# Two MLPs of a small encoder: weight halves made five steps ahead, and one partial product kept in PSUM

## The chip, the core and the metric

The kernel runs on one core of a Trainium2 chip. Five engines work side by side, each through its own instructions in order: TensorE (PE in the profile, its weight loads PEld), VectorE (DVE), ScalarE (ACT), GpSimd (POOL) and SyncE (SP), which here only issues DMA transfers. TensorE writes into PSUM, which has eight banks; DVE and ACT read it from there. The metric is the device time of one execution in microseconds (us). Three runs of the kernel before took 1002.46, 1002.76 and 1003.22 us, so the median is 1002.76 us.

## The reference

Two layers on one sequence of 512 rows with 1024 features, all in fp32. Layer 0 mixes the rows by stick-breaking attention, layer 1 by a gated linear recurrence; each is followed by the same kind of MLP, and a last normalisation ends it:

```python
for layer in range(2):
    h = rms_norm(x, norm_mix[layer])
    x = x + (stick_breaking_attention(h, ...) if layer == 0 else rglru_block(h, ...))
    h = rms_norm(x, norm_mlp[layer])
    u = relu(h @ mlp_w1[layer])            # 1024 -> 4096
    x = x + (u * u) @ mlp_w2[layer]        # 4096 -> 1024
return rms_norm(x, norm_final)
```

The change touches only the two MLPs.

## The kernel before

**Three products for one.** A matrix product in fp32 is made of three in fp32r. An operand `a` is cut into a high half `ah`, which is `a` rounded to fp32r, and a low half `al = a - ah`; the product is `ah*wh + ah*wl + al*wh`. For each tile of weights, then, ACT makes `wh` with a cast and DVE makes `wl` with a subtraction. In the profile these are the groups `ACT CAST wh<-b` and `DVE TENSOR_TENSOR wl<-b,wh`, both of line 798, the line of the helper through which the MLP issues to ACT and DVE.

**Seven products for eight.** Each MLP is cut into four quarters of the 4096 inner features. Quarter 0's first product is done plainly (`squared`); everything after it goes through the fast scheme with seven block products instead of eight, named P1 to P7, for both products of the MLP ("up": 1024 to 4096, "down": 4096 to 1024). The method `run` lists all of it as steps: for quarters 1 to 3, 14 up steps (two parts `p`, seven products each), and for each quarter 14 down steps (seven products, two parts `g` each). That is 98 steps for each MLP. An up step is 24 matmuls of 256 columns (line 1036), a down step 12 matmuls of 512 columns (line 1135).

The down steps come in an order written out by hand:

```python
"mid":  "P1 0 P5 0 P1 1 P2 0 P5 1 P6 0 P6 1 P3 0 P3 1 P7 0 P7 1 P2 1 P4 0 P4 1",
"last": "P1 0 P5 0 P1 1 P2 0 P5 1 P2 1 P6 0 P6 1 P3 0 P3 1 P7 0 P7 1 P4 0 P4 1",
```

"last" is for the fourth quarter of the second MLP alone.

**Sums in PSUM.** Products go to three sums. X takes P1, P6, P7 and P4 one on top of the other, and it is read between them: after P1 it is worth one block of the output, after P6 another, and so on. So TensorE may write P6 only when X has been read after P1. V takes P5 and then P3 in the same manner, W takes P2 alone. In the up steps a sum is one bank and ACT copies it out (`u<-ps`); in the down steps it is two banks (the two halves of a block of rows), and `collect` adds each, scaled, to the output tile `c` (the group `SCALAR_TENSOR_TENSOR c<-ps`). The banks come in a fixed cycle of eight, `BANKS = "oottaazz"` (tags o, t, acc and z, two banks each).

**The operands of the steps.** The weights come in blocks `b11`, `b12`, `b22` in six tiles `b`, loaded by SP's queue one stage ahead at fixed steps (`load`), and `b21` in a tile `raw` just for P2 (`source`). The operand of P5 is `b11 + b12` and that of P6 is this plus `b22`, each added in place by DVE (`DVE b L798`); that of P7 and of P4 is formed by a DMA that adds in flight, issued by POOL (line 1113). `operand` makes `wh` and `wl` from the block, in one of four pairs of tiles. `added` forms a sum, `add(n, ahead)` says how many steps ahead it may be done (P5 two; P6 one in the up steps, none in the down steps, where P6 of part 0 goes by DMA instead), and `make` makes an operand.

**What sets the order.** Within `run`, ACT and DVE execute in exactly the order in which the program writes their instructions (`Ordered`); TensorE too. After each step `i` the program writes `leave(i)`: it reads out the sum of step `i`, and calls `prepare(i + 4)`, which makes the operand that is four steps ahead. For up steps it also squares the result and splits it into halves for the down steps: `u` is combined by DVE (`u<-u`), goes through Relu and Square on ACT, is cast (`sh` or `bh`) and subtracted (`sl` or `bl`). In `leave` of a down step with part 1, the order is: collect the first bank, do the addition for the operand that is `ahead`, collect the second bank, then prepare. Three splits (`waiting`) are put off to fixed places in the down stage. A step's place is its number in the quarter: 0 to 13 up, 14 to 27 down.

**Tiles that matter here.** `wpool` has four buffers each of `wh` and `wl`, and three of `raw`. `raw` is used by P2 inside `run`, and before and after it by the plain slabs (`slab`), among them the first three of the recurrence's input projection, right behind the first MLP.

Of the kernel before, what the change touches and what calls it, by code (L numbers as in the profile page):

```python
# [13 lines left out]
F32R = mybir.dt.float32r  # L14
# [53 lines left out]
def hybrid_encoder(  # L68
# [739 lines left out]
    class Mlp:  # L808
# [28 lines left out]
        def __init__(self, ctx, layer):  # L837
            self.layer, self.sq, self.first = layer, Squares(), None
            self.V, self.A = Ordered(V), Ordered(A)
            self.mp = ctx.enter_context(tc.tile_pool(name=f"mlp{layer}", bufs=2))  # L840
            self.c = [
                self.mp.tile([P, 2, S], F32, tag=f"c{i}", name=f"c{i}", bufs=1) for i in range(4)
            ]
            self.begun, self.a, self.aside = set(), {}, {}
            self.turns = count(4 * layer)
            self.blocks = ExitStack()
            self.bp = self.blocks.enter_context(tc.tile_pool(name=f"blocks{layer}", bufs=2))
            self.u, self.lows, self.s3, self.slots = {}, {}, {}, None

            t = self.bp.tile([P, C // 2 * S + ASIDE], F32R, tag="s41", name="s41", bufs=1)  # L850
            self.s41 = t[:, : C // 2 * S].rearrange("p (k s) -> p k s", s=S)
# [5 lines left out]
        def bank(self):  # L857
            tag = self.BANKS[next(self.turns) % 8]
            return bank("acc" if tag == "a" else tag)
# [231 lines left out]
        def operand(self, raw):  # L1091
            pool = wpools[next(slabs) % len(wpools)]
            wh = pool.tile([P, C, P], F32R, tag="wh", name="wh")
            wl = pool.tile([P, C, P], F32R, tag="wl", name="wl")
            wh, wl = (t.rearrange("p (j k) f -> p j (k f)", j=2) for t in (wh, wl))
            self.A.copy(wh, raw)
            self.V.tensor_tensor(wl, raw, f(wh), ALU.subtract)
            return wh, wl
# [62 lines left out]
        def part(self, sums, name, g, w):  # L1161

            to = self.PRODUCTS[name][3]
            if to not in sums:
                sums[to] = [self.bank() for _ in range(2)]
            for i in range(2):
                self.times(name, g, i, w, sums[to][i], name in ("P1", "P5", "P2"))
# [4 lines left out]
        def run(self, first, between, end):  # L1172
# [47 lines left out]
            def prepare(i):  # L1220
# [5 lines left out]
                if i < len(steps) and steps[i][0] == "down":  # L1226
                    add(i, 0)
                    if waiting and place(i) in (20, 22, 23):
                        self.split_slot(*waiting.pop(0))
# [8 lines left out]
            def load(i):  # L1238
                q4, at = steps[i][1], place(i)
                for do in self.aside.get(i, ()):  # L1240
                    do()

                if i == 0:
                    self.turns = count(2)
                elif at == 0:
                    self.turns = count(4)
                    self.u.clear()
                    del self.a[1]
                elif at == 4:
                    units["down", q4] = self.from_down(q4)  # L1250
                    self.load(units["down", q4], (0, "b11"), (0, "b12"), (1, "b11"))
                elif at == 11:
# [3 lines left out]
                elif at == 22 and q4 < NQ - 1:  # L1256
                    units["up", q4 + 1] = self.from_up(q4 + 1)
                    self.load(units["up", q4 + 1], (0, "b11"), (0, "b12"), (0, "b22"), (1, "b11"))
                elif at == 25 and q4 < NQ - 1:
                    self.load(units["up", q4 + 1], (1, "b12"), (1, "b22"))  # L1260

            def leave(i):

                ahead = i + 4
# [4 lines left out]
                if kind == "down":  # L1269
                    if q4 == 0 and self.s3 and place(i) in self.REPLACE:  # L1270
                        self.replace()
                    apart = p and name == "P2" and self.layer and q4 == NQ - 1
                    if p and not apart:
# [3 lines left out]
                    if p and not apart:  # L1277
# [132 lines left out]
    with ExitStack() as mctx:  # L1410
# [18 lines left out]
        def end(ws, xs):  # L1429
            x_down(0, 0)  # L1430
            for i in range(2):
# [3 lines left out]
                if i == 0:  # L1435
                    for c in range(4, C):
                        feature(c, "zzoo"[c - 4])
# [457 lines left out]
```

## Time and profile before

| | |
|---|---|
| median of three runs | 1002.76 us |
| profiled execution | 1003.18 us |
| its span, first to last instruction | 1001.3 us |
| granted TensorE clock | 0.999 |
| busy: PE, PEld, DVE, ACT, POOL | 98%, 88%, 86%, 71%, 18% of the span |
| up and down steps of quarters 1 to 3, first MLP | 320.8 to 545.1 us of the span |
| the same, second MLP | 766.6 to 991.7 us |

A row of the timeline gives the start, the duration, the engine, the line, the operation, the tiles written and read, how many, and in brackets how long the engine stood idle just before and what ended it. Durations of neighbours overlap a little: an instruction's own time is the distance from its start to that of the next. So two `wl` in a row, shown together as 2.35 us with 1.22 us each, take 1.14 us apiece of DVE's queue, and the matmuls of 512 columns, shown with 379 ns, come every 216 ns.

### The profile page before, as it was taken

Reading aid. Unit: us, or ns where it says so; the run is one execution under the profiler, and the core shown is the slowest. Engines: PE = TensorE matmul, PEld = TensorE weight load, DVE = VectorE, ACT = ScalarE, POOL = GpSimd, SP = SyncE. Lnnn points to the kernel's source line nnn. Section 1 sums busy time; section 2 is a strip of 40 time slices with the busy share of each in tenths; the row PEclk is TensorE's granted clock in tenths of the full one; section 3 lists DMA queues with packets and bytes.
Section 4 is the critical chain, followed back from the end, with each engine's and each line's share of the span. In section 5 each row is a group of like instructions: output and inputs, shape, how many; then the busy total and the mean of one; then the engine's idle time right before and its main releaser. Section 6 shows DMA issues by size and latency. Waiting matters only on the chain.

```text
span 1001.3 us, 15918 instructions
## 1 busy us (share of the span) xinstructions
PE 983.0 (98%) x5836; PEld 884.0 (88%) x5836; DVE 858.0 (86%) x1152; ACT 715.4 (71%) x1110; POOL 176.4 (18%) x243
## 2 busy tenths in 40 slices
PE   9999999999999999999999999999999999999996
PEld 7889999888878988988988888888889989989985
DVE  6888787848898799799799799986887898998898
ACT  6777676836887774774775699975887774874865
POOL 0454444420000011011011220100011111111111
PEclk9999999999999999999999999999999999999999
DMA  7855454537637767777693474446548877977953
GB/s 230 216 146 148 106 153 109 160 117 256 174 87 198 169 160 198 169 163 194 169 239 88 128 191 126 124 157 223 122 95 219 212 142 202 249 141 199 229 107 106
DMA packets 71902, 165.72 MB, mean 166 GB/s; under 512 B 23824, under 2 KB 25104, under 8 KB 71824
## 3 DMA queue, kind: packets, MB, share of 16 engines
q1 hardware_dynamic: 59424, 123.54, 39.4%
q0 software_dynamic: 11680, 40.38, 24.0%
q8 instruction: 46, 0.75, 0.3%
q10 hardware_dynamic: 720, 0.79, 0.2%
q14 instruction: 32, 0.26, 0.1%
HBM read 139.51 MB, written 6.29 MB: 146 GB/s over the span
## 4 chain that ended last, share of the span: by engine, by line
PE 39%; DVE 25%; ACT 22%; issue 8%; DMA 6%; SPq 0%; ACTq 0%; POOL 0%; DVEq 0%; POOLq 0%
PE ps_t L1135 8%; DVE wl L798 6%; ACT wh L798 6%; PE ps_acc L1135 4%; DVE u L798 4%; ACT u L798 3%; PE ps_acc L1036 3%; DVE b L798 3%; PE ps_acc L257 3%; PE ps_acc L259 3%; PE ps_acc L258 2%; PE ps_z L1135 2%; ACT bh L798 2%; DVE c L798 2%; ACT L798 2%
## 5 line engine op out<-in xcount | busy, mean ns | idle before, releaser
L798 ACT CAST wh<-b 128x1024 fp32r<-128x1024 f32 x168 | 173.7, 1048 | 99.6 <-DVE b L798 50.1
L798 DVE TENSOR_TENSOR wl<-b,wh 128x1024 fp32r<-128x1024 f32 x168 | 203.6, 1220 | 38.9 <-ACT wh L798 38.5
L1113 POOL DMA_DIRECT2D b<-in_w_dn x40 | 35.0, 876 | 339.6 <-DVE b L798 153.1
L1036 PE MATMUL ps_z<-xg,wh 128*128 128x256 f32 x384 | 78.2, 277 | 1.0 <-ACT u L798 1.0
L257 PE MATMUL ps_acc<-xg,wh 128*128 128x512 f32 x200 | 79.1, 395 | 0.0
L259 PE MATMUL ps_acc<-xg,wh 128*128 128x512 f32 x200 | 75.8, 379 | 0.0
L258 PE MATMUL ps_acc<-xg,wl 128*128 128x512 f32 x200 | 75.8, 379 | 0.0
L251 DVE TENSOR_TENSOR wl<-raw,wh 128x512 fp32r<-128x512 f32 (+2 forms) x70 | 62.0, 911 | 15.1 <-ACT wh L249 14.8
L798 ACT ACTIVATE u<-u 128x512 f32<-128x512 f32 x100 | 63.2, 632 | 13.3 <-DVE u L798 11.6
L623 DVE TENSOR_TENSOR_SCAN scan<-keep,later 128x128 f32<-128x128 f32 (+1 forms) x64 | 59.3, 929 | 12.9 <-ACT keep L613 6.5
L1036 PE MATMUL ps_z<-xg,wl 128*128 128x256 f32 x240 | 66.0, 275 | 0.0
L1036 PEld LDWEIGHTS ps_z<-xg,wh 128*128 128x128 f32 x384 | 63.5, 192 | 1.7 <-ACT u L798 1.6
L249 ACT CAST wh<-raw 128x512 fp32r<-128x512 f32 (+2 forms) x70 | 50.5, 757 | 19.1 <-PE ps_acc L259 6.8
L627 POOL TENSOR_TENSOR w<-w,scan 128x128 f32<-128x128 f32 (+1 forms) x64 | 51.6, 807 | 53.6 <-DVE scan L623 50.6
L1036 PE MATMUL ps_acc<-xg,wh 128*128 128x256 f32 x288 | 60.5, 275 | 0.0
L798 DVE TENSOR_TENSOR b<-b,b 128x1024 f32<-128x1024 f32 x48 | 58.7, 1223 | 1.3
L798 DVE TENSOR_TENSOR u<-u 128x512 f32<-128x512 f32 (+1 forms) x92 | 54.8, 595 | 2.3 <-ACT u L798 1.0
L1113 POOL DMA_DIRECT2D b<-in_w_up x24 | 20.9, 869 | 196.8 <-DMA b<-in_w_up 84.4
L1036 PE MATMUL ps_acc<-xg,wl 128*128 128x256 f32 x192 | 52.8, 275 | 0.0
L1036 PE MATMUL ps_acc<-low,wh 128*128 128x256 f32 x192 | 52.8, 275 | 0.0
L798 ACT CAST wh<-raw 128x1024 fp32r<-128x1024 f32 x46 | 47.9, 1043 | 4.1 <-PE ps_acc L1135 4.0
L1135 PE MATMUL ps_t<-wh,sl 128*128 128x512 f32 x126 | 48.5, 385 | 1.9 <-DVE sl L798 1.9
(372 smaller groups left out, 3257.9 us busy)
## 6 DMA issues: line engine op xcount, KB each, us to landing
b<-in_w_dn SPq DMA_DIRECT2D x48, 512.0 KB, 5.1
b<-in_w_dn POOLq DMA_DIRECT2D x40, 512.0 KB, 5.5
b<-in_w_up SPq DMA_DIRECT2D x36, 512.0 KB, 4.7
b<-in_w_up POOLq DMA_DIRECT2D x24, 512.0 KB, 5.8
raw<-in_w_m SPq DMA_DIRECT2D x16, 512.0 KB, 4.7
raw<-in_w_dn SPq DMA_DIRECT2D x16, 512.0 KB, 4.9
raw<-in_w_in SPq DMA_DIRECT2D x16, 512.0 KB, 4.2
raw<-in_w_qk SPq DMA_DIRECT2D x12, 512.0 KB, 3.7
```

The source lines that it names most:

```text
L249: A.copy(wh[:, k, :], raw[:, k, :])
L251: V.tensor_tensor(wl[:, k, :], raw[:, k, :], f(wh[:, k, :]), ALU.subtract)
L257: PE.matmul(ps, wh, ah, start=start, stop=False)
L258: PE.matmul(ps, wl, ah, start=False, stop=False)
L259: PE.matmul(ps, wh, al, start=False, stop=stop)
L623: V.tensor_tensor_scan(sc[:, S - n : S][:, ::-1], keep[:, :n][:, ::-1], later[:, S - n :][:, ::-1], 1.0, ALU.mult, ALU.max,)
L627: G.tensor_tensor(wt, wt, sc[:, S - n + 1 : S + 1], ALU.mult)
L798: ins = getattr(self.e, name)(*args, **kwargs)
L1036: PE.matmul(as_read(ps[:, i * HS : (i + 1) * HS]), m, turns_of(y), start=new and i == k == n == 0, stop=i == 1 and k == C // 2 - 1 and n == 2,
L1113: G.dma_start(out=unit[b].rearrange("p j n -> p (j n)"), in_=unit["src"](to), accum_op=ALU.add)
L1135: PE.matmul(ps, m, y[:, jj], start=first and n == 0, stop=last and n == 2, skip_group_check=not new,)
```

## The change

Three things, all inside the MLPs.

1. **Five steps ahead.** From step 14 on (the first up step of quarter 1) `leave(i)` prepares the operand of step `i + 5` and not `i + 4`. The loads of the `b` tiles, from there on, are issued one step sooner. The put-off splits keep the step at which they are written. A fifth pair of tiles for halves is needed: every operand whose number divides by five, from 15 on, uses a fixed pair, `spare`, whose two tiles are two of the three `raw` buffers, held to the end of the MLP. P2's loads are left with one.
2. **W stays in PSUM.** The two banks of the down steps' W are taken once (`kept`) and P2 of all four quarters accumulates there. The collects of P2 in quarters 0, 1 and 2, two each, are gone; only the last quarter's remain.
3. **A plan of banks.** The other six banks are given out by a list written for each quarter (`planned`), X and V of the ups and downs in the order in which they are first used; `self.turns` starts elsewhere for the plain products before, and two transposes behind the first MLP use banks acc and t where it was o twice.

```diff
@@ Mlp.__init__, bank
-            self.turns = count(4 * layer)
+            self.kept, self.growing = None, False
+            self.planned = []
+            self.turns, self.operands, self.spare = count(2 + 2 * layer), count(), None
...
-            tag = self.BANKS[next(self.turns) % 8]
+            tag = self.planned.pop(0) if self.planned else self.BANKS[next(self.turns) % 8]
@@ operand
-            pool = wpools[next(slabs) % len(wpools)]
-            wh = pool.tile([P, C, P], F32R, tag="wh", name="wh")
-            wl = pool.tile([P, C, P], F32R, tag="wl", name="wl")
+            n = next(self.operands)
+            if n >= self.STEPS // 2 and n % 5 == 0:
+                if self.spare is None:
+                    self.spare = [
+                        wpool.tile([P, C, P], F32R, tag="raw", name="spare", bufs=3) for _ in range(2)
+                    ]
+                wh, wl = self.spare
+            else:
+                wh = wpool.tile([P, C, P], F32R, tag="wh", name="wh")
+                wl = wpool.tile([P, C, P], F32R, tag="wl", name="wl")
@@ part
             if to not in sums:
-                sums[to] = [self.bank() for _ in range(2)]
+                if to == "W":
+                    self.kept = self.kept or [self.bank() for _ in range(2)]
+                sums[to] = self.kept if to == "W" else [self.bank() for _ in range(2)]
+            new = name in ("P1", "P5") or name == "P2" and not self.growing
+            self.growing = self.growing or name == "P2" and g == 1
             for i in range(2):
-                self.times(name, g, i, w, sums[to][i], name in ("P1", "P5", "P2"))
+                self.times(name, g, i, w, sums[to][i], new)
@@ run: prepare, load, leave
-                    if waiting and place(i) in (20, 22, 23):
+                    if waiting and place(i) in (21, 23, 24):
...
+                sooner = i >= self.STEPS // 2
                 if i == 0:
-                    self.turns = count(2)
+                    self.planned[:] = "ooatzz"
                 elif at == 0:
-                    self.turns = count(4)
+                    self.planned[:] = ("", "atatooaatoat", "totoaattoa", "oaoattooatat")[q4]
...
-                elif at == 4:
+                elif at == 4 - sooner:
...
-                elif at == 11:
+                elif at == 11 - sooner:
...
-                elif at == 22 and q4 < NQ - 1:
+                elif at == 22 - sooner and q4 < NQ - 1:
...
-                elif at == 25 and q4 < NQ - 1:
+                elif at == 25 - sooner and q4 < NQ - 1:
...
-                ahead = i + 4
+                ahead = i + (5 if i >= self.STEPS // 2 else 4)
...
+                    grows = name == "P2" and q4 < NQ - 1
-                    if p and not apart:
+                    if p and not apart and not grows:
                         self.collect(name, 0, bank[0])
                     if steps[min(ahead, len(steps) - 1)][0] == "down":
                         add(ahead, 0)
-                    if p and not apart:
+                    if p and not apart and not grows:
                         self.collect(name, 1, bank[1])
                     prepare(ahead)
@@ end of the first MLP
-                        feature(c, "zzoo"[c - 4])
+                        feature(c, ("z", "z", "acc", "t")[c - 4])
```

## The prediction

> **What bounds the kernel now.** I read the page first, then the windows of single quarters, TensorE's waits, and last the timelines of TensorE, DVE and ACT in the third quarter of the first MLP, the one from 396.31 us on.
>
> ```profile
> span 1001.3 us, 15918 instructions
> ...
> PE 983.0 (98%) x5836; PEld 884.0 (88%) x5836; DVE 858.0 (86%) x1152; ACT 715.4 (71%) x1110; POOL 176.4 (18%) x243
> ```
>
> ```profile
> core 0: us, PE busy (x) PEld busy (x) DVE busy (x) ACT busy (x) POOL busy (x), PEclk, DMA share, GB/s
> ...
> 396.31:471.05 74.74, 74.33 (x505) 68.96 (x504) 67.25 (x74) 49.13 (x62) 7.85 (x9) 1.00 0.72 177
> ...
> 842.77:917.70 74.93, 74.52 (x506) 69.04 (x505) 69.07 (x77) 49.32 (x62) 10.45 (x12) 1.00 0.84 197
> ```
>
> ```profile
> PE ps_t L1135 <- DVE sl L798: 1.9, 6, 0.3
> PE ps_acc L1135 <- DVE wl L798: 1.4, 3, 0.6
> ...
> PE ps_z L1036 <- ACT u L798: 1.0, 3, 0.6
> ```
>
> TensorE is the bound: it is busy for 74.3 of the 74.7 us of a quarter, at full clock. There is little to win, then. DVE, at 67.3 of 74.7 us, is the next, and its 7.5 us of idle time lie in the first half of the quarter, so in the second half it is a bound of its own. The six waits for `sl` are one in each of the six quarters 1 to 3.
>
> What they cost is seen in the starts of the matmuls around them, and the chain of waits gives the start of P6:
>
> ```profile
> 431.15 0.28 PE L1036 MATMUL ps_z<-xg,wh 128*128 128x256 f32 x1
> ...
> 433.83 0.38 PE L1135 MATMUL ps_t<-wh,bh 128*128 128x512 f32 x1
> ...
> 439.25 0.38 PE L1135 MATMUL ps_t<-wl,sh 128*128 128x512 f32 x1
> 439.95 0.48 PE L1135 MATMUL ps_t<-wh,sl 128*128 128x512 f32 x1 [0.32 <-DVE sl L798]
> 440.27 0.38 PE L1135 MATMUL ps_t<-wh,sh 128*128 128x512 f32 x1
> ...
> 442.21 0.38 PE L1135 MATMUL ps_z<-wh,bh 128*128 128x512 f32 x1
> 442.68 0.48 PE L1135 MATMUL ps_z<-wl,bh 128*128 128x512 f32 x1
> 443.00 0.38 PE L1135 MATMUL ps_z<-wh,bl 128*128 128x512 f32 x1
> ```
>
> ```profile
> 447.91 5.18 PE ps_t L1135 x24
> ...
> 471.22 0.89 PE ps_acc L1036 x8
> ```
>
> 24 matmuls in 5.18 us are 0.216 us each. From 439.25 to 440.27 two take 1.02 us and not 0.43: a wait shown as 0.32 costs 0.59, its own length and 0.27 to get going again. From 442.21 to 443.00 the second wait (P2's `wl`) costs 0.36 likewise. So **0.95 us of each of these quarters, 5.7 us in all**, is what the change can take away at the start of the down stages. The down stage begins at 433.83 (P1 of part 0); P1 of part 1 two steps later at 439.0; P6 at 447.91; the up stage's last step, P4, at 431.15.
>
> **The change, part by part.** *The queue of DVE.* The order on DVE and ACT is the program's, so moving each operand one step ahead moves it past the work of one `leave`. These are DVE's rows from the start of its busy stretch, and ACT's beside them:
>
> ```profile
> 418.30 1.76 DVE L798 TENSOR_TENSOR bl<-u,bh 128x1536 fp32r<-128x1536 f32 x1 [1.47 <-ACT bh L798]
> ...
> 431.42 1.23 DVE L798 TENSOR_TENSOR b<-b,b 128x1024 f32<-128x1024 f32 x1
> ...
> 436.21 0.68 DVE L798 TENSOR_TENSOR u<-u,ps_o 128x512 f32<-128x512 f32 x1
> 436.81 1.22 DVE L798 TENSOR_TENSOR wl<-b,wh 128x1024 fp32r<-128x1024 f32 x1
> 438.06 1.23 DVE L798 TENSOR_TENSOR b<-b,b 128x1024 f32<-128x1024 f32 x1
> 439.21 0.69 DVE L798 TENSOR_TENSOR sl<-u,sh 128x512 fp32r<-128x512 f32 x1
> 440.06 1.42 DVE L798 TENSOR_TENSOR u<-u 128x512 f32<-128x512 f32 x2 [0.17 <-ACT u L798]
> 441.40 1.22 DVE L798 TENSOR_TENSOR wl<-raw,wh 128x1024 fp32r<-128x1024 f32 x1
> ...
> 443.74 2.35 DVE L798 TENSOR_TENSOR wl<-b,wh 128x1024 fp32r<-128x1024 f32 x2
> 446.01 0.74 DVE L798 SCALAR_TENSOR_TENSOR c<-ps_t,rr,c 128x512 f32<-128x512 f32 x1
> 446.68 1.21 DVE L798 TENSOR_TENSOR b<-b,b 128x1024 f32<-128x1024 f32 x1
> ```
>
> ```profile
> 428.67 0.59 ACT L798 COPY u<-ps_z 128x512 f32<-128x512 f32 x1 [0.28 <-PE ps_z L1036]
> ...
> 432.68 1.06 ACT L798 CAST wh<-b 128x1024 fp32r<-128x1024 f32 x1 [0.45 <-DVE b L798]
> ...
> 436.93 1.30 ACT L798 ACTIVATE u<-u 128x512 f32<-128x512 f32 x2 [0.40 <-DVE u L798]
> 438.26 0.62 ACT L798 CAST sh<-u 128x512 fp32r<-128x512 f32 x1
> 438.78 0.59 ACT L798 ACTIVATE u<-ps_z 128x512 f32<-128x512 f32 x1
> ```
>
> At 418.30 DVE has just waited: nothing is queued, and this point hangs on the up steps alone, so it stays. From there I write the queue anew, with 1.14 us for each `wl` and each addition and 0.60 for each `sl` and `u`, from the distances of the rows.
>
> (a) *P4 up.* The operand of P5 (part 0) with its addition is now written before ACT's copy of X after P7, the row at 428.67. The addition of 431.42 goes ahead of one `bl` (1.14) and one `u` (0.60), and the `wl` that followed 418.30 is already made (1.14), so it starts near 428.5. ACT's cast must wait for its end, 429.8, takes 0.95, and the copy runs from 430.75 to 431.3. P4 adds onto the same bank and wants to start at 431.15: 0.2 late, with the 0.27 some **0.5 us** (0 to 1).
>
> (b) *P1 of part 1.* The addition of 438.06 (P5's, part 1) now lies before the `u` of 436.21, which starts at 437.35, and with 0.2 of waits for ACT near 437.5. Between this `u` and the `sl` of 439.21 stands Relu, Square and cast: 436.21 to 438.88, that is 2.67 us. In their shadow DVE had 0.60 + 1.14 + 1.14 us of work; without the addition only 1.74, and it idles for 0.95. `sl` runs then from 440.25 to 440.95, where TensorE, unstopped but for (a), needs it at 439.45 + 0.5. That is 1.0 late, **1.2 us** with the new start (0.9 to 1.5). P2's `wl`, a step early now, is in time: its 0.36 goes.
>
> (c) *P6 of part 0.* P6 adds onto X, so both collects of P1 come first, the rows from 446.01 on. Before, the order was collect, addition for P6 of part 1, collect, then its operand. Now the addition and the operand belong to the `leave` before, in front of the first collect. An addition followed by its cast and `wl` with nothing between stands in the last quarter:
>
> ```profile
> 971.30 1.22 DVE L798 TENSOR_TENSOR b<-b,b 128x1024 f32<-128x1024 f32 x1
> 973.71 1.22 DVE L798 TENSOR_TENSOR wl<-b,wh 128x1024 fp32r<-128x1024 f32 x1 [1.19 <-ACT wh L798]
> ```
>
> So ahead of the collect DVE has the same number of `wl` as before (one more here, one less behind 418.30), one addition more (1.14), and these waits: 1.2 for this cast, 0.95 of (b), 0.6 for the sums behind ACT's Relu and Square of 438.78 to 440.04 (0.17 before, when less `sh` lay behind), 0.7 elsewhere against 0.61. The waits grow by 2.7, the collect starts at 446.01 + 1.14 + 2.7 = 449.85 and ends at 450.6. TensorE reaches P6 at 447.91 - 0.95 + 0.5 + 1.2 = 448.65: 1.95 late, **2.2 us** with the new start. Bounds: 0, if half of the 3.8 us is made good; 3.5, the addition, cast and `wl` in full.
>
> A quarter with the "mid" order: 0.5 + 1.2 + 2.2 - 0.95 = **+2.95 us**, five times 14.7. In the last quarter of the second MLP P2 of part 1 stands before P6, 2.6 us more room, so (c) falls away: 0.5 + 1.2 - 0.95, **+0.5** taken (0 to 1.5), as two shorter waits for `wl` there may go too.
>
> *W kept in PSUM.* Twelve collects go, in six pairs. The pair of this quarter, and ACT's cast beside it:
>
> ```profile
> 467.62 1.40 DVE L798 SCALAR_TENSOR_TENSOR c<-ps_z,rr,c 128x512 f32<-128x512 f32 x2
> 468.94 1.22 DVE L798 TENSOR_TENSOR wl<-b,wh 128x1024 fp32r<-128x1024 f32 x1
> ```
>
> ```profile
> 467.81 1.04 ACT L798 CAST wh<-b 128x1024 fp32r<-128x1024 f32 x1 [3.28 <-DVE b L798]
> ```
>
> The pair takes 1.32 us, but the `wl` behind it needs the cast that ends at 468.85: without the pair DVE would idle there as long. Worth 0. If that cover were gone it would give 1.3 us a quarter, 8 in all.
>
> *The plan of banks.* The trace shows no wait for a bank given anew; the three for `ACT u` are X's, read between two products on one bank. Six banks serve ten sums of a quarter, each first written several steps after its previous reader: 0, at worst 0.6 + 0.27 in each quarter, 5. [...]
>
> *One `raw` buffer.*
>
> ```profile
> raw<-in_w_dn SPq DMA_DIRECT2D x16, 512.0 KB, 4.9
> ```
>
> A load of P2 can now start only when the P2 before is subtracted. These lie five steps (13 us) or more apart, against 4.9 for the load: 0. In the "last" order they are two steps apart and ACT may wait some 2 us, which TensorE needs three steps later: 0, at most 2. Behind the first MLP the second input slab's `raw` is a spare tile, free when P2 of part 1 has run; two steps of 2.6, sixteen transposes and the load's 4.9 with cast and `wl` (2.2) end about together: 0 to 1.
>
> **Sum:** 14.7 + 0.5 = +15.2 on the profiled execution's 1003.18 (its span 1001.3 and 1.9 around it), 1018.4; this execution lies 0.4 above the median of 1002.76, so **1018 us**.
>
> **Rivals.**
>
> *The gaps close (faster).* If weights one step early and 1.3 us less of DVE work a quarter let DVE enter the down stage early enough, all of 5.7 us goes, and with the three waits for `ACT u` (1.0 + 0.8) up to 7.5: 995 to 997. The point: collect (c) must start by 446.9, not 449.85, so 3 us of my 3.8 must be wrong. For it: the same gap in every quarter; against it: the wait in (b) is for `sl`, which is not made earlier. [...]
>
> *Half of it.* (c) comes to nothing because the collects are in time, (a) and (b) stay: 0.75 a quarter, +4.3, 1007.
>
> *Worse.* The single `raw` buffer or SP's queue behind it holds up ACT in each quarter as it may in the last: 2 us more in five of them, 1028.
>
> *No effect.* Both sides cancel, or the fifth pair is not free before the steps need it, so that ACT waits as before: 1002 to 1004.
>
> **How the numbers follow.** Forecast with its own range 1012 to 1022: 0.66. Half: 0.12. Worse: 0.07. No effect: 0.06. Gaps close: 0.09. The range of 8 in 10 reaches to the half case and covers the bounds of (c): 1006 to 1023. About 0.2%, 2 us, is what a measurement of this kernel tells from no change. Faster by more: 0.09; within: 0.05; slower: 0.86.
>
> **What would show it.** Right: in the third quarter's down stage TensorE waits before P6 for `DVE c` with about 2 us, a row that is not there before; `sl` of P1 is waited for longer, P2's `wl` no more; ACT's copy `u` stops P4 up; a quarter of 74.7 becomes 77.7; DVE idles about 3.5 us between its 418.30 and the first collect. Wrong: quarters under 74.7, the row `b<-b,b` still behind the first `c<-ps_t`, or the added time lying outside quarters 1 to 3.

## The result and the profile after

The changed kernel takes 1027.39 us, the median of four runs (1025.44 to 1031.72), beside 1002.78 for the kernel before. The ratio is 1.0253, with a 95% interval from 1.0236 to 1.027. The profiled execution took 1025.44, with a span of 1023.5 us; the kernel before had 1001.3, so the two traces differ by 22.2. The page after:

```profile
span 1023.5 us, 15900 instructions
...
PE 989.1 (97%) x5836; PEld 888.9 (87%) x5836; DVE 852.6 (83%) x1140; ACT 712.3 (70%) x1110; POOL 176.1 (17%) x243
```

DVE has twelve instructions less (1140 for 1152), the collects of W, and is busy 5.4 us less. TensorE has the same 5836 matmuls, and its busy time has grown by 6.1, so not all of the loss stands in the rows as idle time.

The windows of quarters 1 and 2, of the first MLP and then of the second. Two of the four stand in the prediction as they were before, 74.74 and 74.93:

```profile
core 0: us, PE busy (x) PEld busy (x) DVE busy (x) ACT busy (x) POOL busy (x), PEclk, DMA share, GB/s
320.17:400.27 80.10, 75.42 (x505) 69.33 (x504) 66.64 (x72) 51.07 (x65) 7.81 (x9) 1.00 0.70 170
400.27:478.07 77.80, 74.82 (x505) 69.11 (x504) 66.36 (x72) 48.61 (x62) 7.85 (x9) 1.00 0.70 170
779.26:861.51 82.25, 77.03 (x505) 70.44 (x504) 68.32 (x74) 51.32 (x65) 9.69 (x12) 0.98 0.77 184
861.51:939.75 78.24, 74.83 (x506) 69.11 (x505) 67.71 (x75) 48.68 (x62) 10.42 (x12) 1.00 0.81 188
```

Quarter 2 is 3.06 and 3.31 longer than before. Quarter 1 is longer still, by 4.63 and 6.04 (75.47 and 76.21 before), and in one of the four the granted clock is 0.98.

TensorE's waits, in us in total, how often, and the longest:

```profile
PE ps_t L1144 <- DVE c L798: 4.1, 2, 2.0
PE ps_acc L1144 <- DVE c L798: 4.1, 2, 2.0
PE ps_acc L1038 <- ACT u L798: 3.7, 6, 0.8
PE ps_o L1144 <- DVE c L798: 2.7, 2, 2.0
PE ps_t L1038 <- ACT u L798: 1.9, 2, 1.0
PE ps_t L1144 <- ACT sh L798: 1.3, 2, 0.6
PE ps_acc L1144 <- ACT sh L798: 1.3, 2, 0.6
PE ps_o L1144 <- ACT sh L798: 1.3, 2, 0.6
...
PE ps_o L1038 <- ACT u L798: 1.0, 2, 0.7
```

Line 1144 is the down step now, 1038 the up step. The six rows of `c` and `sh` are new. Five of the six waits for `c` are 2.03 long and stand before P6, one in each quarter with the "mid" order; the six for `sh` stand before P1 of part 1; and the waits for `ACT u`, three of 1.0 in all before, are ten with 6.6. The late start at P2's `wl` is gone. (The rows for `wl` that remain are not P2's: they stand in the two quarters 0, which are still four ahead. A wait for `c` of 0.67 is new in the last quarter.)

DVE in the third quarter of the first MLP, the one that the prediction rewrote (its 418.30 is the 422.22 here):

```profile
422.22 1.76 DVE L798 TENSOR_TENSOR bl<-u,bh 128x1536 fp32r<-128x1536 f32 x1 [1.48 <-ACT bh L798]
...
437.65 0.69 DVE L798 TENSOR_TENSOR sl<-u,sh 128x512 fp32r<-128x512 f32 x1 [0.29 <-ACT sh L798]
438.61 1.23 DVE L798 TENSOR_TENSOR wl<-b,wh 128x1024 fp32r<-128x1024 f32 x1 [0.27 <-ACT wh L798]
439.87 1.23 DVE L798 TENSOR_TENSOR b<-b,b 128x1024 f32<-128x1024 f32 x1
...
444.30 0.69 DVE L798 TENSOR_TENSOR sl<-u,sh 128x512 fp32r<-128x512 f32 x1 [0.87 <-ACT sh L798]
445.46 1.42 DVE L798 TENSOR_TENSOR u<-u 128x512 f32<-128x512 f32 x2 [0.47 <-ACT u L798]
...
450.28 1.22 DVE L798 TENSOR_TENSOR b<-b,b 128x1024 f32<-128x1024 f32 x1
452.66 1.23 DVE L798 TENSOR_TENSOR wl<-b,wh 128x1024 fp32r<-128x1024 f32 x1 [1.17 <-ACT wh L798]
453.80 1.40 DVE L798 SCALAR_TENSOR_TENSOR c<-ps_t,rr,c 128x512 f32<-128x512 f32 x2
```

Both collects now stand behind the addition of 450.28, its cast on ACT and its half. The waits in brackets add up to 3.07 (0.78 before). The first collect starts 31.58 after the `bl` of 422.22, where it was 27.71 before: 3.87 later, 1.14 of it the third addition and 2.73 waiting. (The brackets alone give 2.29 of the 2.73, since they leave out the stretch by which neighbouring rows overlap, and waits too short to be listed.)

### The profile page after: what moved, and what is told of

Read it like the earlier page. It is cut to its first block, busy times and chain, and to the rows that moved or that the text cites. A ratio compares the mean times of both kernels' runs of the same rounds, so it can differ in the third digit from the quotient of the medians.

```text
span 1023.5 us, 15900 instructions
## 1 busy us (share of the span) xinstructions
PE 989.1 (97%) x5836; PEld 888.9 (87%) x5836; DVE 852.6 (83%) x1140; ACT 712.3 (70%) x1110; POOL 176.1 (17%) x243
## 4 chain that ended last, share of the span: by engine, by line
PE 42%; DVE 23%; ACT 18%; issue 9%; DMA 6%; SPq 0%; ACTq 0%; POOL 0%; DVEq 0%; POOLq 0%
DVE wl L798 6%; ACT wh L798 4%; PE ps_t L1144 4%; DVE b L798 3%; PE ps_acc L257 3%; PE ps_acc L259 3%; PE ps_acc L258 3%; ACT u L798 3%; PE ps_o L1144 3%; PE ps_o L1038 3%; PE ps_acc L1144 3%; DVE u L798 2%; PE ps_t L1038 2%; DVE c L798 2%; DVE bl L798 2%
## 5 line engine op out<-in xcount | busy, mean ns | idle before, releaser
L798 ACT CAST wh<-b 128x1024 fp32r<-128x1024 f32 x137 | 142.6, 1048 | 89.2 <-DVE b L798 62.9
L798 DVE TENSOR_TENSOR wl<-b,wh 128x1024 fp32r<-128x1024 f32 x137 | 166.3, 1219 | 44.0 <-ACT wh L798 42.4
L798 ACT CAST spare<-b 128x1024 fp32r<-128x1024 f32 x31 | 32.4, 1045 | 33.5 <-DVE b L798 21.2
L1038 PE MATMUL ps_t<-xg,wh 128*128 128x256 f32 x240 | 47.2, 276 | 1.9 <-ACT u L798 1.9
L1038 PE MATMUL ps_acc<-xg,wh 128*128 128x256 f32 x224 | 46.4, 277 | 2.1 <-ACT u L798 2.1
L798 DVE TENSOR_TENSOR spare<-b,spare 128x1024 fp32r<-128x1024 f32 x31 | 37.8, 1219 | 12.1 <-ACT spare L798 12.1
L798 ACT CAST wh<-raw 128x1024 fp32r<-128x1024 f32 x43 | 44.8, 1044 | 3.5 <-DMA raw<-in_w_dn 2.0
L798 DVE TENSOR_TENSOR wl<-raw,wh 128x1024 fp32r<-128x1024 f32 x35 | 42.6, 1218 | 1.7 <-ACT wh L798 1.6
L617 POOL TENSOR_SCALAR_AFFINE_SELECT w<-w 128x128 f32<-128x128 f32 x64 | 32.3, 504 | 67.4 <-ACT w L612 67.1
L798 DVE TENSOR_TENSOR bl<-u,bh 128x1024 fp32r<-128x1024 f32 (+2 forms) x26 | 33.8, 1302 | 11.8 <-ACT bh L798 11.8
```

Source lines behind the costliest of these rows:

```text
L617: G.affine_select(t, t, pattern=[[-1, P]], compare_op=ALU.is_gt, fill=0.0, base=0, channel_multiplier=1,)
L798: ins = getattr(self.e, name)(*args, **kwargs)
L1038: PE.matmul(as_read(ps[:, i * HS : (i + 1) * HS]), m, turns_of(y), start=new and i == k == n == 0, stop=i == 1 and k == C // 2 - 1 and n == 2,
```

## The experiments

The theory: the whole loss lies in the order of DVE's and ACT's queues, since an operand made five steps ahead is written in front of the read-outs and splits of one more step. The rivals: the banks (two of eight held for W, and the plan for the rest), the single `raw` buffer, and separate causes that can be put right one by one. All times are medians beside runs of the kernel before on the same chip (1002.5 to 1002.7).

| kernel | us | ratio to before, 95% |
|---|---|---|
| four ahead, W kept, plan of banks | 1002.81 | 1.0004 (0.9995 to 1.0012) |
| five ahead alone | 1024.77 | 1.0223 (1.0209 to 1.0237) |
| five ahead, P1's collects put back in front | 1024.27 | 1.0218 (1.0203 to 1.0234) |
| five ahead from quarter 2 on | 1020.50 | 1.0178 (1.0157 to 1.0198) |
| before, with the fifth pair | 1005.17 | 1.0025 (1.0014 to 1.0035) |
| five ahead, P5's addition one step later | 1021.27 | 1.0183 (1.0162 to 1.0204) |
| before, with step (c) alone | 1021.01 | 1.0185 (1.017 to 1.02) |
| five ahead, ACT's copy of X put back in front | 1033.86 | 1.0311 (1.0297 to 1.0325) |
| three instructions moved, five ahead | 1017.83 | 1.0154 (1.0138 to 1.0169) |
| before, one `sl` moved | 999.32 | 0.9968 (0.9958 to 0.9979) |
| four ahead, W kept, one `sl` moved | 999.48 | 0.9972 (0.9962 to 0.9983) |

### One half of the change, then the other

First W and the banks without the five steps (the changed kernel with):

```diff
-            if n >= self.STEPS // 2 and n % 5 == 0:
+            if False:
...
-                    if waiting and place(i) in (21, 23, 24):
+                    if waiting and place(i) in (20, 22, 23):
...
-                sooner = i >= self.STEPS // 2
+                sooner = 0
...
-                ahead = i + (5 if i >= self.STEPS // 2 else 4)
+                ahead = i + 4
```

> This kernel keeps the sum of P2 in PSUM and the new plan of banks, but prepares operands four steps ahead as before, with no fifth pair, and loads the blocks at the old places. Theory (the order of DVE's and ACT's queues with operands five steps ahead is the whole loss): 1002.8 within 1, a quarter of the first MLP 74.7, no wait of P6 for DVE c above 0.1, the six waits for DVE sl (0.3 shown) and the three for P2's wl as in the kernel before. The step of the prediction that puts the twelve collects at 0 says the same; if their 1.3 us a quarter count after all, up to 8 less, 995. Rival (the plan of banks makes a bank be awaited, or holding two of eight for W does): 1008 or more, with waits for a bank's reader at the first matmul of a sum, 0.9 in each of five or six quarters.

Measured: 1002.81, no difference from before. The quarter and the waits of this kernel:

```profile
394.88:469.62 74.74, 74.34 (x506) 68.97 (x504) 66.01 (x72) 49.07 (x62) 7.86 (x9) 1.00 0.71 177
```

```profile
PE ps_t L1038 <- ACT u L798: 1.0, 3, 0.6
...
PE ps_acc L1144 <- DVE sl L798: 0.6, 2, 0.3
```

The quarter is 74.74, as before to the hundredth. DVE is busy 66.01 in it for 67.25, so the two collects (1.32) really are gone, and TensorE gets nothing for them. The waits for `u` and for `sl` (three such rows, on three tags of banks) are those of before. (So are three for `wl`, 1.4 in all; the expectation calls them P2's, but two of them lie in quarter 0 and one in the last quarter of the second MLP.)

Then the five steps without W and the banks (P2 is collected in each quarter, the banks are dealt in the old cycle, also at three places that aren't printed here):

```diff
-                    grows = name == "P2" and q4 < NQ - 1
+                    grows = False
...
-                if to == "W":
-                    self.kept = self.kept or [self.bank() for _ in range(2)]
-                sums[to] = self.kept if to == "W" else [self.bank() for _ in range(2)]
-            new = name in ("P1", "P5") or name == "P2" and not self.growing
-            self.growing = self.growing or name == "P2" and g == 1
+                sums[to] = [self.bank() for _ in range(2)]
+            new = name in ("P1", "P5", "P2")
...
-                    self.planned[:] = ("", "atatooaatoat", "totoaattoa", "oaoattooatat")[q4]
+                    self.turns = count(4)
```

> The other half alone: operands five steps ahead with the fifth pair and the earlier loads, but P2's sums collected in every quarter and the banks dealt in the old cycle. Theory: as the changed kernel, 1025 to 1029, with the wait of P6 for DVE c of 2 us in five quarters; the pair of collects again fills an idle time of DVE and costs nothing. Rival (the banks or W carry the loss): back towards 1003. A third way: the pair of collects lies on the path now that DVE is late, 1.3 more a quarter, 1033.

Measured: 1024.77, a little under the lower end of what was expected. The quarter is 77.77 and the waits for `c` are there again:

```profile
PE ps_t L1144 <- DVE c L798: 10.5, 6, 2.0
```

So the loss is that of the five steps; W and the banks have no part in it that these runs show. Of the 2.6 between the medians, the traces show 1.4, and that is there before anything changed runs: at 27 us of the span this trace is already 1.8 ahead. The rest isn't explained; the changed kernel's own runs differ by 6.3.

### The place of the collects

The changed kernel with the addition and the operand for P6 of part 1 written behind P1's collects, in the five quarters with the "mid" order:

```diff
+                    held = q4 and kind_of(q4) == "mid"
+                    if held and place(i) == 15:
+                        return
                     if p and not apart and not grows:
                         self.collect(name, 0, bank[0])
...
                         self.collect(name, 1, bank[1])
+                    if held and place(i) == 16:
+                        add(ahead - 1, 0)
+                        prepare(ahead - 1)
                     prepare(ahead)
```

> The changed kernel with one thing put back: in the five quarters of the mid order the addition and the operand for P6 of part 1 are written behind P1's two collects. Theory A (DVE is late by an addition, a cast and a weight half as a whole, and the wait stands at whatever comes next): the 2.2 at P6 of part 0 goes, but 1.5 to 2 of it comes back at P6 of part 1 and at P3 and P4 of part 0, for sl, c or wl, each under 1 us; 1022 to 1025, lower by the two dips of the clock, which no gap of 2 us sets off any more. Theory B (only the place of the collects is wrong): 2.2 in each of five quarters and the dips go, 1011 to 1013.

Measured: 1024.27, as theory A has it, though one of the waits is longer than it said. No wait is 2 us long any more, and there are still five for `c`, each of 1.2:

```profile
PE ps_o L1144 <- DVE c L798: 3.0, 3, 1.2
PE ps_t L1144 <- DVE c L798: 2.4, 2, 1.2
...
PE ps_acc L1144 <- DVE c L798: 1.2, 1, 1.2
```

(The row of 3.0 holds a sixth, shorter one of the last quarter.) They stand before P3 of part 0 now, two steps on, and wait for the collects of V after P5, which come behind the operand that was moved. In the starts of the matmuls the 2.27 has become 0.45 at P6 of part 1, 1.44 before P3 and 0.28 before P4, together 2.17. The quarter is 77.68 for 77.80, so by the waits next to nothing is won. What is gone in this trace is two falls of the clock (its mean is 0.999 here, 0.995 in the trace after; 3.4, below); and 1.6 of that is lost again at the projection behind the first MLP, where TensorE now waits 0.6 and 1.0 for `xg`.

Step (c) alone, in the kernel before, four ahead:

```diff
+                    late = q4 and place(i) == 16 and not (self.layer and q4 == NQ - 1)
+                    if late:
+                        add(ahead, 0)
+                        prepare(ahead)
                     if p and not apart:
                         self.collect(name, 0, bank[0])
-                    if steps[min(ahead, len(steps) - 1)][0] == "down":
+                    if not late and steps[min(ahead, len(steps) - 1)][0] == "down":
                         add(ahead, 0)
                     if p and not apart:
                         self.collect(name, 1, bank[1])
-                    prepare(ahead)
+                    if not late:
+                        prepare(ahead)
```

> The kernel before, four ahead, with step (c) alone: in the five mid quarters the addition and the operand for P6 of part 1 are written ahead of P1's two collects. By the rows of before the first collect starts at 449.4 and not at 446.0 (addition 1.14, cast 1.05, half 1.14) and ends at 450.2, where P6 stands ready at 447.9: a wait of 2.3 to 2.5 each, 12 in all, 1014 to 1015 by that alone. If a gap of 2 us lets the granted clock fall to 0.5, some of the five gaps do so here too, 1.6 each, 1015 to 1019 and a mean clock under 0.998. Rival (the wait at P6 needs the late DVE of five ahead): under 1 us each, 1003 to 1007.

Measured: 1021.01, above the highest figure expected for it. One row of the waits has changed against before:

```profile
PE ps_t L1135 <- DVE c L798: 12.8, 5, 2.7
```

Five waits of 2.5 to 2.7, at the place of step (c), with weights four steps ahead. With the new starts they are 2.8 to 2.9 each, 14.0 together. The clock falls four times in this trace (its mean is 0.992), which costs 6.4 more; and the trace is 1.8 shorter than before in its first 27 us, ahead of anything that was changed. That makes the 18.5 by which the two spans differ, to 0.1. One of the four falls:

```profile
375.30:378.67 3.37, 3.37 (x9) 2.70 (x8) 3.37 (x5) 2.13 (x4) 0.00 (x0) 0.50 1.04 171
```

Nine matmuls take 3.37 us here, beginning 1.2 after TensorE went on; at 0.216 each they would take 1.94.

### The other steps, one at a time

P5's addition one step later, so that in the down stage it comes behind P2's sum `u` again, for step (b) (the up steps' P5 is moved with it):

```diff
-                if ahead > (5 if far else 2 if name == "P5" else what[0] == "up"):
+                if ahead > (5 if far else (1 if i >= self.STEPS // 2 else 2) if name == "P5" else what[0] == "up"):
```

> The changed kernel with P5's addition on DVE one step later (one step ahead of its operand and not two), so that in the down stage it comes behind the sum u of P2, as in the kernel before. Theory: step (b) is this addition: the wait of P1 of part 1 for sh (0.99 with the new start) falls, but DVE's later work keeps its chain of addition, cast and half, so P6 still waits about 2.0; in all 2 to 4 less than the changed kernel, 1024 to 1025. Rival (this addition is the root of (c) too): P6's wait falls by the 1.14 of the addition as well, 8 to 12 less, 1016 to 1019.

Measured: 1021.27, lower than theory and higher than rival. The rows side with the theory: the waits for `c` are 1.9 each and not under 1, and the quarters shrink by 0.56 (77.24 for 77.80 in the first MLP, 77.68 for 78.24 in the second).

```profile
400.93:478.17 77.24, 74.83 (x506) 69.18 (x505) 66.30 (x72) 48.62 (x62) 7.85 (x9) 1.00 0.70 171
```

Five times 0.56 are 2.8, what the theory said. In the traces the span is 3.8 less: these 2.8, and 3.4 for the clock, which doesn't fall here (its mean is 0.998), less 2.4 at the projection behind the first MLP, where TensorE waits 1.5 and 1.0 for `xg`. So the addition is a part of (b), some 0.4 of 1.2, and of (c) only 0.17; this much was really won.

ACT's copy of X after P7 put back in front of P5's operand, for step (a):

```diff
-                prepare(ahead)
+                held = p and i >= self.STEPS // 2
+                if held and name == "P7":
+                    prepare(ahead - 1)
+                if not (held and name == "P3"):
+                    prepare(ahead)
```

> The changed kernel with step (a) alone undone: the operand with addition for P5 of part 0 is written behind ACT's copy of X after P7 and not in the step ahead of it; all else is five ahead. Theory A (the order is a zero sum: with two operands and an addition in one step, the Relu, Square and cast that P1 of part 1 hangs on come later by that much): the wait of P4 up (0.45 to 1.17 in six quarters) goes, the wait of P1 of part 1 for sh or sl grows from 0.99 to 2.5 or 3, in all 2 to 4 more than the changed kernel, 1029 to 1032. Theory B (each wait stands for itself): 0.83 less in each of six quarters, 1022 to 1023.

Measured: 1033.86, the worst kernel of all, past the range of theory A in the direction that it gave. P4 up waits no more, and P1 of part 1 waits as long as A said. The first of three such rows (the others have 5.2 and 5.1):

```profile
PE ps_acc L1144 <- ACT sh L798: 5.8, 2, 2.9
```

The waits for `sh` were 0.63 each and are 2.3 to 2.9. Of the three puttings-back, then, two show the same thing: DVE and ACT execute one list between the up and the down stage, and a wait that is taken from one place of it comes out at another. Only P5's addition gave something, 0.56 a quarter.

Five ahead only from quarter 2 on (42 steps in, instead of 14; the fifth pair, the loads and the places of the splits likewise), for the additional waits in quarter 1:

```diff
-                ahead = i + (5 if i >= self.STEPS // 2 else 4)
+                ahead = i + (5 if i >= self.STEPS * 3 // 2 else 4)
```

> The changed kernel with five ahead (fifth pair, earlier loads, later places of the waiting splits) only from the down stage of quarter 1 plus one up stage on, that is from the start of quarter 2; quarter 1 runs four ahead. Theory (every mid quarter with five ahead loses about 3 of its own, and the quarter in which four becomes five loses 1 to 2 more at three waits for ACT u): quarter 1 is as before, 75.5 and 76.2, and the additional waits for ACT u stand in quarter 2 now; 6 to 8 under the changed kernel, 1019 to 1022. Rival (the additional waits of quarter 1 belong to quarter 1 itself, where the first MLP's halves are put back, and not to the switch): quarter 2 stays at 77.8, 1017 to 1018.

Measured: 1020.50, as the theory has it. Quarter 1 and quarter 2 of the first MLP, then of the second:

```profile
320.76:395.96 75.20, 74.72 (x506) 69.04 (x504) 64.71 (x70) 49.71 (x63) 7.81 (x9) 1.00 0.68 162
395.96:477.04 81.08, 76.86 (x506) 70.40 (x504) 68.38 (x74) 50.61 (x64) 7.91 (x10) 0.98 0.69 167
779.27:855.53 76.26, 74.97 (x505) 69.12 (x504) 65.84 (x72) 49.58 (x63) 9.62 (x11) 1.00 0.76 174
855.53:937.22 81.69, 77.04 (x506) 70.40 (x504) 69.99 (x77) 50.71 (x64) 10.54 (x13) 0.98 0.81 185
```

Quarter 1 is as before. Quarter 2 has grown from 77.80 and 78.24 to 81.08 and 81.69; less the 1.7 that one fall of the clock takes in each, it is 1.6 and 1.8 longer than a quarter that comes after one of five ahead. The additional waits go with the quarter in which four becomes five, and with them the long wait of P4 up, 1.0 in both. ACT in the changed kernel's quarter 1 shows how:

```profile
329.79 1.05 ACT L798 CAST spare<-b 128x1024 fp32r<-128x1024 f32 x1 [3.47 <-DMA b<-in_w_up]
330.74 0.58 ACT L798 COPY u<-ps_acc 128x512 f32<-128x512 f32 x1
```

The cast for P4, a step early, waits for the DMA that adds to its block, which POOL issued at 323.60, after waiting for DVE's `wl`, and which landed 6.1 later; the copy of X, which TensorE waits for at 330.8, stands behind it.

The fifth pair without five steps, in the kernel before:

```diff
-            pool = wpools[next(slabs) % len(wpools)]
-            wh = pool.tile([P, C, P], F32R, tag="wh", name="wh")
-            wl = pool.tile([P, C, P], F32R, tag="wl", name="wl")
+            n = next(self.operands)
+            if n >= self.STEPS // 2 and n % 5 == 0:
+                if self.spare is None:
+                    self.spare = [
+                        wpool.tile([P, C, P], F32R, tag="raw", name="spare", bufs=3) for _ in range(2)
+                    ]
+                wh, wl = self.spare
+            else:
+                wh = wpool.tile([P, C, P], F32R, tag="wh", name="wh")
+                wl = wpool.tile([P, C, P], F32R, tag="wl", name="wl")
```

> The kernel before, four ahead, with only the fifth pair in two of the three raw buffers, so that one raw buffer is left in the MLPs. Theory (one raw buffer costs nothing, as the prediction has it, but for the last quarter and the projection after the first MLP): 1002.5 to 1004. Rival (a load that waits for the one buffer stops SP's queue or ACT in each quarter): 2 more in each of five quarters, 1012.

Measured: 1005.17, 2.7 slower than before and 1.2 above what was expected. It isn't in each quarter. One place is the projection behind the first MLP, where the second slab's load finds no free `raw`. ACT before:

```profile
538.23 1.05 ACT L249 CAST wh<-raw 128x1024 fp32r<-128x1024 f32 x1 [1.54 <-PE ps_t L1135]
540.82 1.05 ACT L249 CAST wh<-raw 128x1024 fp32r<-128x1024 f32 x1 [1.54 <-PE ps_z L1135]
```

and with the fifth pair:

```profile
538.00 1.04 ACT L249 CAST wh<-raw 128x1024 fp32r<-128x1024 f32 x1 [5.41 <-PE ps_z L1142]
542.93 1.05 ACT L249 CAST wh<-raw 128x1024 fp32r<-128x1024 f32 x1 [3.89 <-PE ps_z L1429]
```

The second cast is 4.9 after the first instead of 2.6, DVE subtracts the half at 544.0, and TensorE waits 1.57 for the normalised input that DVE makes behind it. With the new starts the projection takes 1.9 more than before. The other place is the last quarter, where the second P2 comes two steps after the first: four waits, 3.0 in all with the new starts, for 0.3 before. (At P1 of part 1, over six quarters, this kernel gets 1.0 back, and its first 27 us are 0.7 shorter.) In the changed kernel itself the last quarter shows none of it and the projection 0.6; where the experiments brought TensorE sooner to the projection, the wait came back, as told above.

### One instruction moved, and what that is worth

Block 2 of part 1 is read by P4 of part 1 alone, the last step of the down stage. Its low half is nevertheless made in front of P2's sum `u`, on whose Relu, Square and cast P1 of part 1 hangs. In the kernel before:

```diff
                 if op:
                     self.V.tensor_tensor(cut(u[at]), x, y, op)
+                if lows and name == "P2":
+                    self.V.tensor_tensor(*lows.pop(), ALU.subtract)
...
-                        if p:
+                        if p and at == 2:
+                            h, l = (a[:, :, at, :] for a in self.places(p))
+                            self.A.copy(h, u[at])
+                            lows.append((l, u[at], f(h)))
+                        elif p:
                             self.split_slot(p, u[at], at)
```

> The kernel before with one DVE instruction moved: the low half sl of block 2 of part 1 (the split of P7's result in the up stage) is written behind the sum u of P2 and not ahead of it; ACT's cast stays. If it is the queue of DVE that makes P1 of part 1 wait, the u of P2 starts 0.6 earlier and with it Relu, Square, cast and the sl that P1 waits for: of the 0.95 a quarter some 0.6 goes in each of six quarters, 999 to 1000. Rival (the wait hangs on ACT's chain of Relu, Square, cast with other work of ACT between): unchanged, 1002.8.

Measured: 999.32, the fastest kernel here; the interval ends at 0.9979. TensorE at the start of the down stage, at the place quoted before:

```profile
436.71 0.38 PE L1135 MATMUL ps_t<-wl,sh 128*128 128x512 f32 x1
437.18 0.48 PE L1135 MATMUL ps_t<-wh,sl 128*128 128x512 f32 x1
437.50 0.38 PE L1135 MATMUL ps_t<-wh,sh 128*128 128x512 f32 x1
```

Two matmuls take 0.79, not 1.02, and P2's wait is 0.1 for 0.36. A quarter takes 74.24 and 74.43, each 0.50 less, as the expectation has it but for 0.1. Of 0.95 some 0.5 is gone, six times. That is the gap that the change was about, halved without any deeper buffer.

The same with W kept and the plan of banks, four ahead (this edit and the first one together):

> The kernel with four ahead, W kept in PSUM and the new plan of banks, plus the one moved instruction sl of block 2 behind P2's sum u. Theory (W and the banks are worth nothing, the moved sl is worth 3.2): 999 to 1000. Rival (the pair of collects that is gone gives DVE room once the moved sl has closed the waits at the start of the down stage): 995 to 998.

Measured: 999.48, so W is worth nothing here either.

Last, the three edits that took something off, together in the changed kernel (collects in front, P5's addition later, this `sl`):

> The changed kernel, five ahead throughout, with the three edits together that each took something off alone: the collects of P1 ahead of the addition and operand for P6 of part 1, P5's addition one step later, and the sl of block 2 behind P2's sum. Theory (DVE and ACT have the queue of four ahead only if all is put back, the rest is lost at P4 up, P3 and P4 of part 0): 0.3 and 0.55 in each of five quarters and 0.5 in each of six off, no gap of 2 us and so no dip of the clock: 1014 to 1018. Rival (these three are all that was wrong, five ahead then closes what it was to close): under 1002.

Measured: 1017.83, at the upper end of the theory. A quarter is 76.67 and 77.12, 1.1 under the changed kernel and 1.9 and 2.2 over the one before. What remains in it is P4 up and the wait of P3 for the collects of V, 1.2 as shown; outside it the switch in quarter 1 and two waits at the projection. So the three account for some 10 of 24.6; the rest belongs to five ahead with this list.

## Why the prediction was wrong

The direction was as forecast, and so were the three places and the mechanism at them. The size was not: +15.2 was forecast, and it is 22.2 in the profiled execution (24.6 in the medians). Three steps failed: the clock and the quarter of the switch had no term, and (a), the wait of P4 up, was sized from one quarter for all six. The terms, measured over the starts of the matmuls so that the new start is in them:

| term | predicted | measured in the trace after |
|---|---|---|
| (c) P6 behind the collects, five times | 5 x 2.2 = 11.0 | 2.27 each, 11.4 |
| (b) P1 of part 1, less the 0.95 of before, six times | 6 x 0.25 = 1.5 | 1.20 each, for 0.94 to 1.08 before: +1.1 |
| (a) P4 up, six times | 6 x 0.5 = 3.0 | 0.56, 0.58, 0.99, 1.04, 1.20, 1.27: 5.6 |
| the switch from four to five in quarter 1 | no term | 3.7 for 2.0 before: +1.7 |
| the clock | no term | two falls of 1.7: +3.4 |
| rest of the last quarter | -0.25 | waits of 0.8 for `rt` and 0.8 for two `wl` are gone, one of 0.9 for `c` has come: -0.7 |
| quarter 0 and the projection | 0 | -0.8 and +0.6: -0.2 |
| sum | 15.2 | 22.3 |

**(b) and (c) were right to the tenth.** One addition more and 2.73 of waits put the first collect 3.87 later after its `bl`; the prediction had 3.84, with 2.7 of waits, and its single waits (1.2, 0.95, 0.6, 0.7) stand in the rows above as 1.17, 0.87, 0.47 and 0.56. Only the 0.95 that it took off for the waits of before was read from one quarter; the other five had up to 1.08. TensorE at P6 and at P1 of part 1, after:

```profile
452.28 0.38 PE L1144 MATMUL ps_acc<-spare,sl 128*128 128x512 f32 x1
454.69 0.45 PE L1144 MATMUL ps_t<-wh,bh 128*128 128x512 f32 x1 [2.03 <-DVE c L798]
454.98 0.38 PE L1144 MATMUL ps_t<-wl,bh 128*128 128x512 f32 x1
```

```profile
443.31 0.38 PE L1144 MATMUL ps_acc<-wh,bl 128*128 128x512 f32 x1
444.32 0.48 PE L1144 MATMUL ps_t<-wh,sh 128*128 128x512 f32 x1 [0.64 <-ACT sh L798]
...
445.37 0.38 PE L1144 MATMUL ps_t<-wh,sh 128*128 128x512 f32 x1
```

452.28 to 454.98 is 2.70 for two matmuls of 0.216: 2.27 lost. 443.31 to 445.37 is 2.06 for four: 1.20 lost. What is waited for is `sh` with most of it, ACT's cast, and `sl` with the rest; the prediction named `sl`, the next link of the same chain.

**(a) was mis-sized.** In the quarter that it was read from it is 0.56 for 0.5. Taking that for all six was the mistake: in the second MLP the `bl` from which the queue is written comes 22.38 after the quarter's start and not 21.95 (883.89 less 861.51, and 422.22 less 400.27), behind the transposes that DVE does there, and P4 up costs 0.4 more; in quarter 1 it costs 1.2 to 1.3, and the experiment that begins in quarter 2 moved this with the switch.

**The switch had no term.** The prediction worked out a quarter that is five ahead from its start and used it five times; the quarter in which two operands have to be made for one step was not looked at by itself. It cost 1.7 in the two quarters 1 together. The experiment that begins in quarter 2 moved these waits with it.

**The clock had no term either**, and it is the largest miss. The prediction saw TensorE at full clock before and priced each wait by its length and the new start alone. After two of the five waits for `c` the clock falls, here after the third (three windows of equal length, columns as above):

```profile
529.50:532.91 3.41, 1.38 (x7) 0.92 (x6) 2.44 (x3) 3.35 (x4) 0.81 (x1) 1.00 0.80 124
532.91:536.33 3.42, 3.42 (x10) 2.70 (x9) 3.42 (x5) 0.95 (x2) 0.07 (x1) 0.50 0.95 149
536.33:539.74 3.41, 3.41 (x17) 2.98 (x17) 3.41 (x6) 2.15 (x4) 0.00 (x0) 1.00 0.19 37
```

TensorE is back at work by 532.5. In the second window, at half clock, stand ten matmuls, in the third seventeen. That is also the larger part of the 6.1 by which TensorE's busy time grew. Over its whole length each run has a mean clock: the four runs of the changed kernel had 0.992 to 0.996 (0.999 before), so the number of falls seems to differ from run to run, and the slowest run, 1031.72, had the lowest clock.

**What was put at nothing.** W and the plan of banks: confirmed, twice. One `raw` buffer: both places were named rightly. In the changed kernel the projection lost 0.6, within its bounds (0 to 1), and the last quarter nothing; with four ahead both went over their bounds (1.9 for at most 1, and 2.7 more than before for at most 2). Rival "worse" gave 1028, near the result, by luck: its mechanism, 2 us more in each quarter from the `raw` buffer, isn't in the trace. Too few buffers were a small part of the gap that repeats at most: with the fifth pair alone the gap at P1 and P2 lost 1.0 of its 6.1 us, with five steps a quarter became 3 us longer, and moving one subtraction closed half of the gap.

The range ended at 1023: its upper end took the bound of (c), 3.5, and none for a quarter or a fall of the clock that had no term.

## What to carry to other kernels

When engines execute their lists in the order of the program, making an operand one step earlier puts its whole chain (addition, cast, subtraction, and the waits between them) ahead of every read-out of that step; write the queue anew from a point that doesn't move, as (b) and (c) did, and do it once for each kind of stage, the transition too. DVE's idle share of 10% was no room here, since it consisted of waits inside chains like this one. Before buffering deeper, look for the instruction in front of the late chain whose result is needed last: here one of 0.6 us, moved behind one other, was worth 3.

## What the runs showed of the hardware that was not expected

The granted clock falls to 0.50 after some of TensorE's waits of 2 us. In the trace after there are five such waits, of 2.03 or 2.04, all for `c` in front of P6. After the third and the fourth, which end at 532.50 and 836.44, the clock's own record has 0.50 for 3.41 us, from 532.91 and from 836.70; the first of these stretches is shown above. Within it the matmuls of 512 columns start 0.43 apart (533.09 to 535.65), for 0.216 at full clock. Eight of them fill 3.41 us and would otherwise have taken 1.73, so a fall costs up to 1.7, an estimate from these rows.

After the other three of the five the clock stays at 1.00. The second of the five, in the quarter before, is 2.03 long, and the matmul that it holds up starts at 454.69:

```profile
451.00:454.41 3.41, 1.66 (x8) 1.12 (x6) 2.25 (x3) 2.83 (x4) 0.75 (x2) 1.00 0.63 85
454.41:457.82 3.41, 3.13 (x15) 2.79 (x16) 3.41 (x6) 0.88 (x2) 0.77 (x1) 1.00 0.93 149
```

What sets the waits that were followed by a fall apart from the others is left open here.

The mean clocks of the profiled executions fit this. Five of the thirteen have waits of 2.0 us or more: 0.995 for the changed kernel, 0.995 for five ahead alone, 0.996 for five ahead from quarter 2 on, 0.992 for step (c) alone (waits of 2.5 to 2.7) and 0.993 with ACT's copy in front (up to 2.9). In the other eight the longest wait is 1.9 (P5's addition one step later), and the clock is 0.998 or 0.999. Runs of one kernel differ: five ahead alone had 0.995 in three of its four runs and 0.999 in one. For two of the four runs with P1's collects in front, whose waits end at 1.2 in the trace, the mean clock is 0.996, and where it fell in them no trace shows.

In these traces, then, a wait of 2 us can be dearer than two of 1 us: in the trace after, two of the five waits of 2.03 or 2.04 were followed by a fall, and none of the waits for `u`, of up to 1.0, was.
